# Second layer of a two-layer decoder: stick-breaking queries and keys projected first, scored at every fourth step, GpSimd's small operations on DVE and ACT

## The chip, the cores and the metric

The kernel runs on one core of a Trainium2 chip. The core has a matrix engine (TensorE; its rows in a profile are PE for the matmuls and PEld for the loads of the stationary operand), a vector engine (VectorE, DVE), a scalar engine (ScalarE, ACT), GpSimd (POOL) and SyncE (SP), which here only issues the loads of the weights. Each engine runs its own instructions in the order in which the program lists them, and waits on semaphores for the others. The metric is the device time of one execution, in microseconds (us).

## The reference

Two post-norm layers over 256 positions with a model width of 2048, float32 in and out, causal. Each layer computes `x = LN(alpha*x + mixer(x))` and then `x = LN(alpha*x + relu(x W1)^2 W2)` with a hidden width of 8192. The mixer of the first layer (even) is a sliding-window attention beside a dilated one. The change is in the mixer of the second layer (odd):

```
h = x @ w_in                               # 2048 -> 3*1024 + 512 + 256 + 32
qc, kc, vc, cq, ckv, kr = split(h)
# C: stick-breaking attention, 16 heads of 64
z = qc kc^T / 8 ; strict causal mask
log_keep = log_sigmoid(-z); after = reverse exclusive cumsum of log_keep over keys
oc = exp(log_sigmoid(z) + after) @ vc
# D: latent attention, 16 heads, 64 + 32 (rotary) wide
q  = rms(cq) @ w_uq ; kv = rms(ckv) @ w_ukv
od = softmax([q_nope, rope(q_rope)] . [k_nope, rope(kr)] / sqrt(96)) @ v
y = concat(oc, od) @ w_out
```

## The kernel before

**Precision.** Every large product runs as three float32r products: a weight block `w` is split into `w_hi` (a rounding copy, on ACT, line 120) and `w_lo = w - w_hi` (on DVE, line 121), the activations likewise, and hi*hi, lo*hi and hi*lo are summed in PSUM.

**Units.** All weights come through one `Stream`, in the order in which `plan` (line 380) lists them, as units of 128 x 1024 numbers (512 KB; 384 KB for the queries of D). `Stream.next` hands out one unit; ahead of that it emits the loads (up to five units ahead of the splits) and the split of the unit that stands three later. So each unit costs ACT one `w_hi`, DVE one `w_lo`, and PE 12, 16 or (for `ukv`) 18 matmuls.

**Projections.** `project` (line 833, through `ws`, line 305) computes 512 output columns, transposed, from eight units into four PSUM banks named `acc`; `v_c` (line 894, through `as_`, line 341) computes the values of C from eight units into two such banks; `uq` (line 947) computes the D queries of four heads from two units into four banks, `ukv` (line 980) the D keys and values of eight heads from two units into four banks. There are four `acc` banks in all. A bank is handed on when it has been read: after `project` and `uq` by `join` (line 334), an ACT copy `xfull` and a DVE addition for each bank; after `v_c` by ACT copies; after `ukv` by copies, of which two banks go to ACT and two to DVE (lines 1002 to 1013).

**Attention between the units.** After each unit `pump` (line 189) runs one small piece: a function of the list `late`, a step of a side generator, and one attention step (`attn_step`, line 213). An attention job holds eight heads (half of C or half of D: C0, D0, C1, D1). A step at which a pair of heads is scored emits `qk` (line 682, PE, into two PSUM banks named `sc`, of which there are two) and the mask additions of both heads (DVE; line 1046 for C, 1027 for D). The later stages of a head follow one step apart: for C three ACT activations (`soft`, lines 1050 to 1052), the DVE scans (`sums`, lines 1057 to 1061), an ACT exponential (line 1064); for D maxima on DVE, exponentials on ACT, a division on DVE. Some steps after the scoring, `flip` transposes the weights on PE (line 260) and `weigh` multiplies them with the values (lines 279 and 281). The next pair may be scored two steps later: `self.turn = i + 2` (line 239).

**Order in the second layer** (`odd`, line 841). First the latents `cq` and `ckv, kr`; then values of C0, queries of C0, two units of D queries, keys of C0; from here C0 is scored. Then two units of D queries, values of C1, `ukv`; from here D0 is scored. Then queries of C1, two units of D queries, keys of C1; C1 is scored. Then two units of D queries, `ukv`; D1 is scored. The output projection follows: 16 units for C0 and D0, eight for C1, eight for D1.

**GpSimd.** After each `uq`, `rotate` (line 955) turns the rotary rows of two heads: two DVE multiplications and one addition on GpSimd (line 959). After each `ukv`, GpSimd copies the shared rotary key beside each pair's keys (line 1008, four copies).

Of the kernel before, what the change touches and what calls it, by code (L numbers as in the profile page):

```python
# [15 lines left out]
ALU = mybir.AluOpType  # L16
# [3 lines left out]
S = 256  # L20
D = 2048
# [45 lines left out]
class Stream:  # L67


    def __init__(self, k):  # L70
        self.k = k
        self.units = []
        self.nd = 0
        self.ns = 0
        self.nu = 0
        self.live = {}
# [74 lines left out]
class Job:  # L151


    def __init__(self, name, n, per, score, stages, value, lag, y):
        self.name, self.n, self.per, self.lag = name, n, per, lag
        self.score, self.stages, self.value, self.y = score, stages, value, y
        self.left = n // 2
        self.out = []
        self.s = {}
        self.pt = {}  # L160
        self.o = None


class Trunk:
# [48 lines left out]
    def attn_step(self):  # L213
# [24 lines left out]
        self.todo.popleft()  # L238
        self.turn = i + 2
        scs = [self.ps.tile([P, 384], F32, name="sc", bufs=2) for _ in pair]  # L240
# [139 lines left out]
    def plan(self):  # L380
# [18 lines left out]
        w.block(wi, 0, KT, 3584, 288)  # L399
        w.block(wi, 0, KT, 2048, 512)  # L400
        w.block(wi, 0, KT, 0, 512)
        self.plan_uq(0, 0)
        w.block(wi, 0, KT, 1024, 512)
        self.plan_uq(0, 1)
        w.block(wi, 0, KT, 2048 + 512, 512)
        self.plan_ukv(0)
        w.block(wi, 0, KT, 512, 512)
        self.plan_uq(1, 0)
        w.block(wi, 0, KT, 1024 + 512, 512)
        self.plan_uq(1, 1)  # L410
        self.plan_ukv(1)
        wo = a["odd_w_out"][0]
# [428 lines left out]
    def odd(self):  # L841
# [23 lines left out]
        self.side.append(self.latents(zq, zk, kr))  # L865
        vc0 = self.v_c()
        qc0 = self.project(512, "c", 0.125)
        self.finish_side()
        q0 = self.uq()
        kc0 = self.project(512, "c")  # L870
        c0 = self.job_c("C0", qc0, kc0, vc0, self.y_at)
        q0 += self.uq()
        vc1 = self.v_c()
        d0 = self.job_d("D0", q0, self.ukv(), self.y_at)
        qc1 = self.project(512, "c", 0.125)
        q1 = self.uq()
        kc1 = self.project(512, "c")
        c1 = self.job_c("C1", qc1, kc1, vc1, self.x_slot)
        q1 += self.uq()
        d1 = self.job_d("D1", q1, self.ukv(), lambda k: self.x_slot(4 + k))  # L880
        st = self.new_stats()
        for jobs, first, stats in (((c0, d0), True, None), ((c1,), False, None), ((d1,), False, st)):
# [3 lines left out]
            for c in range(4):  # L886
                end = stats is not None and c == 3
                o = self.as_(xs, len(xs), 512, hold=2 if end else 0)
                if not end:
                    self.add_res(o, c, first, stats)  # L890
                    self.pump()
        return (o, c, False), st

    def v_c(self):
# [52 lines left out]
    def uq(self):  # L947
# [7 lines left out]
        def rotate(q):  # L955
            tmp = self.at.tile([P, 2, S], F32, name="rtmp", bufs=1)
            nc.vector.tensor_tensor(tmp[64:96], q[96:128], sn, op=ALU.mult)
            nc.vector.tensor_tensor(q[64:96], q[64:96], cs, op=ALU.mult)
            nc.gpsimd.tensor_tensor(q[64:96], q[64:96], tmp[64:96], op=ALU.add)

# [19 lines left out]
    def ukv(self):  # L980
# [21 lines left out]
        for f in range(4):  # L1002
            k = self.tile2("d")
            src = banks[f // 2][:, (f % 2) * S:(f % 2) * S + S]
            copy = nc.vector.tensor_copy if f > 1 else nc.scalar.copy
            copy(k[0:64, 0, :], src[0:64, :])
            copy(k[0:64, 1, :], src[64:128, :])
            nc.gpsimd.tensor_copy(k[64:96], self.krT[64:96, :].unsqueeze(1).to_broadcast([32, 2, S]))
            ks.append(k)
# [8 lines left out]
    def job_d(self, name, qs, kv, y):  # L1018
# [13 lines left out]

        job = Job(name, 8, 1, score, (bias, power, divide), value, 5, y)
        self.queue(job)
        return job

    def job_c(self, name, qs, ks, vs, y):
# [30 lines left out]

        job = Job(name, 8, 1, score, (mask, soft, sums, power), value, 6, y)
        self.queue(job)  # L1070
# [97 lines left out]
```

## Time and profile before

| what | value |
|---|---|
| median of 3 runs | 2216.11 us (2214.33 to 2218.61) |
| the profiled execution, own time | 2213.81 us |
| its span, first to last instruction | 2212.0 us |
| mean granted TensorE clock | 0.996 |
| busy, share of the span | PE 98%, PEld 83%, DVE 63%, ACT 48%, POOL 3% |
| the stretch 1185 to 1470 us (the mixer of the second layer) | DVE 9.8 of 10 us busy in 1250 to 1280 and again in 1360 to 1390 |

The profile names instructions by line of the kernel, engine and tile; a wait is put down to the instruction that released it. Tables by windows give the busy time of each engine in each stretch, with the number of instructions in brackets, and at the end the granted TensorE clock, the share of the DMA engines and the moved GB/s. A timeline row gives the start in us, the duration in us, the instruction, and in brackets the idle time of the engine before it and what ended it. The engines overlap neighbouring instructions, so what an instruction costs its engine is read from the distance between two starts.

### The profile page before, as it was taken

To read this page: it belongs to the slowest core of one execution; us is meant where nothing else is said; L and a number is where in the kernel's file an instruction comes from. 1 tells how busy PE (TensorE), PEld (TensorE's weight loads), DVE (VectorE), ACT (ScalarE), POOL (GpSimd) and SP (SyncE) were. 2 spreads that over 40 slices of the span, in tenths; PEclk is the share of its full clock that TensorE was granted. 3 is DMA by queue.
4 is the path that set the end of the run, shared out by engine and by line. 5 is a ranking of instruction groups with operands and counts; after the bars stand their busy time and mean duration, and the time that the engine had idled before them with its cause. 6 is when DMAs were issued, how large, how long until landed. Compare 5 with 4: busy or idle time off the path is not lost.

```text
span 2212.0 us, 30040 instructions
## 1 busy us (share of the span) xinstructions
PE 2177.3 (98%) x11603; PEld 1829.7 (83%) x11604; DVE 1403.4 (63%) x1903; ACT 1058.6 (48%) x1525; POOL 61.0 (3%) x85
## 2 busy tenths in 40 slices
PE   9999999999999999999999999999999999999997
PEld 7888887888888888888888787778888888888885
DVE  5766465775565465556578888878645555655665
ACT  4555453554454354354345566645535534534542
POOL 0000000000000000000022101000000000000001
PEclk9999999999999999999999999999999999999998
DMA  7445554555565555555557544456555556555652
GB/s 265 151 139 158 155 169 158 194 191 200 181 199 192 191 180 198 191 184 188 192 160 212 155 126 144 143 200 212 197 191 177 196 192 189 171 208 173 202 187 105
DMA packets 224320, 399.07 MB, mean 180 GB/s; under 512 B 12778, under 2 KB 56512, under 8 KB 223408
## 3 DMA queue, kind: packets, MB, share of 16 engines
q1 hardware_dynamic: 221760, 387.30, 53.0%
q0 software_dynamic: 2416, 9.84, 1.6%
q8 instruction: 91, 1.49, 0.3%
q14 instruction: 53, 0.43, 0.1%
HBM read 395.00 MB, written 2.10 MB: 180 GB/s over the span
## 4 chain that ended last, share of the span: by engine, by line
PE 61%; issue 31%; DVE 5%; DMA 1%; ACT 1%; POOL 0%; SPq 0%; POOLq 0%; DVEq 0%; ACTq 0%
PE acc L326 14%; PE acc L372 9%; PE acc L374 9%; PE acc L373 9%; PE acc L327 7%; PE sc L326 3%; DVE w_lo L121 2%; PE sc L327 1%; PE o L326 1%; PE pt L326 1%; PE sc L688 1%; PE pt L260 1%; PE o L279 1%; DMA raw<-in_even_w_in 1%; PE o L327 1%
## 5 line engine op out<-in xcount | busy, mean ns | idle before, releaser
L121 DVE TENSOR_TENSOR w_lo<-raw,w_hi 128x1024 fp32r<-128x1024 f32 (+2 forms) x748 | 890.9, 1204 | 610.9 <-ACT w_hi L120 606.7
L120 ACT CAST w_hi<-raw 128x1024 fp32r<-128x1024 f32 (+2 forms) x748 | 759.2, 1028 | 765.3 <-PE acc L374 458.8
L326 PE MATMUL acc<-x,w_hi 128*128 128x512 f32 x1824 | 652.5, 401 | 3.6 <-DVE x L515 3.3
L327 PE MATMUL acc<-x,w_lo 128*128 128x256 f32 x1824 | 512.4, 281 | 0.7 <-DVE w_lo L121 0.7
L326 PEld LDWEIGHTS acc<-x,w_hi 128*128 128x128 f32 x1824 | 343.2, 188 | 89.8 <-issue 3.8
L374 PE MATMUL acc<-w_hi,h_lo 128*128 128x512 f32 x1016 | 398.5, 392 | 0.0
L373 PE MATMUL acc<-w_lo,h_hi 128*128 128x512 f32 x1016 | 398.2, 392 | 0.0
L372 PE MATMUL acc<-w_hi,h_hi 128*128 128x512 f32 x1016 | 396.1, 390 | 0.0
L327 PEld LDWEIGHTS acc<-x,w_lo 128*128 128x128 f32 x1824 | 345.4, 189 | 1.4 <-DVE w_lo L121 1.0
L372 PEld LDWEIGHTS acc<-w_hi,h_hi 128*128 128x128 f32 x1016 | 190.7, 188 | 42.6
L373 PEld LDWEIGHTS acc<-w_lo,h_hi 128*128 128x128 f32 x1016 | 190.8, 188 | 42.4
L374 PEld LDWEIGHTS acc<-w_hi,h_lo 128*128 128x128 f32 x1016 | 190.9, 188 | 40.0
L326 PE MATMUL sc<-x,w_hi 128*128 128x512 f32 x512 | 185.4, 396 | 0.0
L327 PE MATMUL sc<-x,w_lo 128*128 128x256 f32 x512 | 143.4, 280 | 0.0
L372 PE MATMUL acc<-w_hi,x 128*128 128x256 f32 (+2 forms) x400 | 136.3, 341 | 0.3 <-DVE x L514 0.2
L374 PE MATMUL acc<-w_hi,x 128*128 128x256 f32 (+2 forms) x400 | 133.2, 333 | 0.0
L373 PE MATMUL acc<-w_lo,x 128*128 128x256 f32 (+2 forms) x400 | 133.0, 332 | 0.1
L326 PEld LDWEIGHTS sc<-x,w_hi 128*128 128x128 f32 x512 | 96.1, 188 | 23.0
L338 ACT ACTIVATE xfull<-acc 128x256 f32<-128x256 f32 x130 | 49.7, 385 | 126.5 <-PE acc L327 108.9
L327 PEld LDWEIGHTS sc<-x,w_lo 128*128 128x128 f32 x512 | 96.7, 189 | 0.0
L326 PE MATMUL o<-x,w_hi 128*128 128x512 f32 x256 | 95.6, 396 | 0.0
L326 PE MATMUL pt<-x,w_hi 128*128 128x512 f32 x256 | 95.6, 396 | 0.0
(197 smaller groups left out, 2088.6 us busy)
## 6 DMA issues: line engine op xcount, KB each, us to landing
raw<-in_mlp_w SPq DMA_DIRECT2D x512, 512.0 KB, 3.8
raw<-in_even_w_in SPq DMA_DIRECT2D x92, 512.0 KB, 4.2
raw<-in_odd_w_in SPq DMA_DIRECT2D x56, 512.0 KB, 3.6
raw<-in_odd_w_out SPq DMA_DIRECT2D x32, 512.0 KB, 3.4
raw<-in_even_w_out SPq DMA_DIRECT2D x24, 512.0 KB, 3.7
gb_rows<-in_ln_g POOLq DMA_DIRECT2D x3, 1024.0 KB, 4.8
gb_rows<-in_ln_b POOLq DMA_DIRECT2D x3, 1024.0 KB, 6.8
raw<-in_odd_w_uq SPq DMA_DIRECT2D x8, 384.0 KB, 4.0
```

Source lines behind the costliest of these rows:

```text
L120: nc.scalar.copy(h, r)
L121: nc.vector.tensor_tensor(l, r, h.bitcast(F32), op=ALU.subtract)
L260: nc.tensor.transpose(pt[:, b * P:(b + 1) * P], st[:, u * 384 + b * P:u * 384 + (b + 1) * P], self.ident)
L279: nc.tensor.matmul(o[rows, :], v, w[:, 0:S], start=first, stop=False, skip_group_check=True)
L326: nc.tensor.matmul(banks[f], hi[:, c:c + P], both, start=first, stop=False, skip_group_check=True)
L327: nc.tensor.matmul(banks[f][:, S:2 * S], lo[:, c:c + P], xh, start=False, stop=last, skip_group_check=True)
L338: nc.scalar.activation(t, bank[:, S:2 * S], AF.Copy, scale=scale)
L372: nc.tensor.matmul(outs[t], xh[:, ts], hi[:, c:c + width], start=first, stop=False, skip_group_check=True)
L373: nc.tensor.matmul(outs[t], xh[:, ts], lo[:, c:c + width], start=False, stop=False, skip_group_check=True)
L374: nc.tensor.matmul(outs[t], xl[:, ts], hi[:, c:c + width], start=False, stop=last, skip_group_check=True)
L688: nc.tensor.matmul(sc[:, cols], q[:, qs], k[:, ks], start=True, stop=True, skip_group_check=True)
```

## The change

The second layer's loop body becomes one function, `heads(half, ...)`, called twice. In each half the queries and keys of C are projected first, C is queued for scoring, then come the values of C, both groups of D queries (four units in a row), and `ukv`; then D is queued. The list of weight units is put in the same order. `Job` gets a `pace`: pairs of C are scored four steps apart, pairs of D three (the first layer's jobs keep two). The rotary addition goes from GpSimd to DVE, and the copies of the rotary key from GpSimd to ACT.

```diff
--- before.py
+++ after.py
@@ -151,8 +151,8 @@
 class Job:
 
 
-    def __init__(self, name, n, per, score, stages, value, lag, y):
-        self.name, self.n, self.per, self.lag = name, n, per, lag
+    def __init__(self, name, n, per, score, stages, value, lag, y, pace=2):
+        self.name, self.n, self.per, self.lag, self.pace = name, n, per, lag, pace
         self.score, self.stages, self.value, self.y = score, stages, value, y
         self.left = n // 2
         self.out = []
@@ -236,7 +236,7 @@
                 both = self.at.tile([P, 768], F32, name="S", bufs=self.s_bufs)
                 job.s[h], job.s[h + 1] = both[:, 0:384], both[:, 384:768]
         self.todo.popleft()
-        self.turn = i + 2
+        self.turn = i + job.pace
         scs = [self.ps.tile([P, 384], F32, name="sc", bufs=2) for _ in pair]
         self.qk(scs, [job.score(g, u) for g in pair])
         for j, (g, sc) in enumerate(zip(pair, scs)):
@@ -397,18 +397,12 @@
         wi = a["odd_w_in"][0]
         w.block(wi, 0, KT, 3072, 512)
         w.block(wi, 0, KT, 3584, 288)
-        w.block(wi, 0, KT, 2048, 512)
-        w.block(wi, 0, KT, 0, 512)
-        self.plan_uq(0, 0)
-        w.block(wi, 0, KT, 1024, 512)
-        self.plan_uq(0, 1)
-        w.block(wi, 0, KT, 2048 + 512, 512)
-        self.plan_ukv(0)
-        w.block(wi, 0, KT, 512, 512)
-        self.plan_uq(1, 0)
-        w.block(wi, 0, KT, 1024 + 512, 512)
-        self.plan_uq(1, 1)
-        self.plan_ukv(1)
+        for half in range(2):
+            for c0 in (0, 1024, 2048):
+                w.block(wi, 0, KT, c0 + half * 512, 512)
+            self.plan_uq(half, 0)
+            self.plan_uq(half, 1)
+            self.plan_ukv(half)
         wo = a["odd_w_out"][0]
         for k0s in ((0, 8), (4,), (12,)):
             for c in range(4):
@@ -863,21 +857,8 @@
             nc.vector.tensor_tensor(kr[:, t, 64:96], kt_[:, t, :], ks[:, t, :], op=ALU.add)
         self.pump()
         self.side.append(self.latents(zq, zk, kr))
-        vc0 = self.v_c()
-        qc0 = self.project(512, "c", 0.125)
-        self.finish_side()
-        q0 = self.uq()
-        kc0 = self.project(512, "c")
-        c0 = self.job_c("C0", qc0, kc0, vc0, self.y_at)
-        q0 += self.uq()
-        vc1 = self.v_c()
-        d0 = self.job_d("D0", q0, self.ukv(), self.y_at)
-        qc1 = self.project(512, "c", 0.125)
-        q1 = self.uq()
-        kc1 = self.project(512, "c")
-        c1 = self.job_c("C1", qc1, kc1, vc1, self.x_slot)
-        q1 += self.uq()
-        d1 = self.job_d("D1", q1, self.ukv(), lambda k: self.x_slot(4 + k))
+        c0, d0 = self.heads(0, self.y_at, self.y_at)
+        c1, d1 = self.heads(1, self.x_slot, lambda k: self.x_slot(4 + k))
         st = self.new_stats()
         for jobs, first, stats in (((c0, d0), True, None), ((c1,), False, None), ((d1,), False, st)):
             for j in jobs:
@@ -890,6 +871,17 @@
                     self.add_res(o, c, first, stats)
                     self.pump()
         return (o, c, False), st
+
+    def heads(self, half, yc, yd):
+
+        qc = self.project(512, "c", 0.125)
+        kc = self.project(512, "c")
+        vc = []
+        c = self.job_c(f"C{half}", qc, kc, vc, yc)
+        vc += self.v_c()
+        self.finish_side()
+        q = self.uq() + self.uq()
+        return c, self.job_d(f"D{half}", q, self.ukv(), yd)
 
     def v_c(self):
         o = self.as_(self.xT, KT, 512)
@@ -956,7 +948,7 @@
             tmp = self.at.tile([P, 2, S], F32, name="rtmp", bufs=1)
             nc.vector.tensor_tensor(tmp[64:96], q[96:128], sn, op=ALU.mult)
             nc.vector.tensor_tensor(q[64:96], q[64:96], cs, op=ALU.mult)
-            nc.gpsimd.tensor_tensor(q[64:96], q[64:96], tmp[64:96], op=ALU.add)
+            nc.vector.tensor_tensor(q[64:96], q[64:96], tmp[64:96], op=ALU.add)
 
         kt = 0
         for u in range(2):
@@ -1005,7 +997,7 @@
             copy = nc.vector.tensor_copy if f > 1 else nc.scalar.copy
             copy(k[0:64, 0, :], src[0:64, :])
             copy(k[0:64, 1, :], src[64:128, :])
-            nc.gpsimd.tensor_copy(k[64:96], self.krT[64:96, :].unsqueeze(1).to_broadcast([32, 2, S]))
+            nc.scalar.copy(k[64:96], self.krT[64:96, :].unsqueeze(1).to_broadcast([32, 2, S]))
             ks.append(k)
         for b in range(2):
             v = self.tile2("d")
@@ -1030,7 +1022,7 @@
         def value(h, u, blk):
             return vs[h // 4][:, blk, (h % 4) * HD:(h % 4) * HD + HD]
 
-        job = Job(name, 8, 1, score, (bias, power, divide), value, 5, y)
+        job = Job(name, 8, 1, score, (bias, power, divide), value, 5, y, pace=3)
         self.queue(job)
         return job
 
@@ -1066,7 +1058,7 @@
         def value(h, u, blk):
             return vs[h // 4][:, blk, (h % 4) * HD:(h % 4) * HD + HD]
 
-        job = Job(name, 8, 1, score, (mask, soft, sums, power), value, 6, y)
+        job = Job(name, 8, 1, score, (mask, soft, sums, power), value, 6, y, pace=4)
         self.queue(job)
         return job
 
```

How this moves instructions is seen at three places. The first is SP, which issues the weight loads in the order of the units, from the values and projections of C0 on (`odd_w_uq` are the D queries, `odd_w_ukv` the D keys and values, the other `odd_w_in` blocks the projections of C). Before:

```order
L92 DMA raw<-in_odd_w_in 128x2x512 x16
L92 DMA raw<-in_odd_w_uq 128x2x384 x2
L92 DMA raw<-in_odd_w_in 128x2x512 x8
L92 DMA raw<-in_odd_w_uq 128x2x384 x2
L92 DMA raw<-in_odd_w_in 128x2x512 x8
L92 DMA raw<-in_odd_w_ukv 128x1024 x2
L92 DMA raw<-in_odd_w_in 128x2x512 x8
L92 DMA raw<-in_odd_w_uq 128x2x384 x2
L92 DMA raw<-in_odd_w_in 128x2x512 x8
L92 DMA raw<-in_odd_w_uq 128x2x384 x2
L92 DMA raw<-in_odd_w_ukv 128x1024 x2
```

Now:

```order
L92 DMA raw<-in_odd_w_in 128x2x512 x24
L92 DMA raw<-in_odd_w_uq 128x2x384 x4
L92 DMA raw<-in_odd_w_ukv 128x1024 x2
L92 DMA raw<-in_odd_w_in 128x2x512 x24
L92 DMA raw<-in_odd_w_uq 128x2x384 x4
L92 DMA raw<-in_odd_w_ukv 128x1024 x2
```

The eight-unit projections that stood between the groups of D queries are gone from there: four units of queries and two of `ukv` now follow each other.

The second place is DVE behind the second `uq` of the first half, from its joins (`d<-acc,xfull`) on. `rtmp` and `d<-d,rope_f` are the rotation, `sb_a` and `S<-S,sb_a` one head's `sums`, `w_lo` the split of a later unit, `S<-masks,sc` the mask additions. Before (C0's first pair has been scored one step earlier):

```order
L339 SCALAR_TENSOR_TENSOR d<-acc,xfull 128x256 x4
L957 TENSOR_TENSOR rtmp<-d,rope_f 32x512
L958 TENSOR_TENSOR d<-d,rope_f 32x512
L121 TENSOR_TENSOR w_lo<-raw,w_hi 128x1024 x2
L957 TENSOR_TENSOR rtmp<-d,rope_f 32x512
L958 TENSOR_TENSOR d<-d,rope_f 32x512
L1057 SCALAR_TENSOR_TENSOR sb_a<-S,sb_a 128x384
L1060 SCALAR_TENSOR_TENSOR sb_a<-sb_a 128x128
L1060 SCALAR_TENSOR_TENSOR sb_a<-sb_a 128x256
L1061 TENSOR_TENSOR S<-S,sb_a 128x384
L1046 TENSOR_TENSOR S<-masks,sc 128x384 x2
```

Now, behind the joins of the first of the half's two `uq` (lines are those of the changed kernel: 949 to 951 the rotation, 1049 to 1053 the sums, here of C0's fifth head):

```order
L339 SCALAR_TENSOR_TENSOR d<-acc,xfull 128x256 x4
L949 TENSOR_TENSOR rtmp<-d,rope_f 32x512
L950 TENSOR_TENSOR d<-d,rope_f 32x512
L951 TENSOR_TENSOR d<-d,rtmp 32x512
L286 TENSOR_TENSOR y<-o,y 128x256
L121 TENSOR_TENSOR w_lo<-raw,w_hi 128x1024 x2
L949 TENSOR_TENSOR rtmp<-d,rope_f 32x512
L950 TENSOR_TENSOR d<-d,rope_f 32x512
L951 TENSOR_TENSOR d<-d,rtmp 32x512
L1049 SCALAR_TENSOR_TENSOR sb_a<-S,sb_a 128x384
L1052 SCALAR_TENSOR_TENSOR sb_a<-sb_a 128x128
L1052 SCALAR_TENSOR_TENSOR sb_a<-sb_a 128x256
```

The next row is the last of that head's sums, and then come the four joins of the half's second `uq`: they stand behind two rotations with their additions and one head's sums. Behind them come a rotation, the sums of the sixth head, two `w_lo`, another rotation and the masks of C0's fourth pair, and only then DVE's copies out of the banks of `ukv`.

The third place is ACT at that `ukv`: `d<-acc` are its copies out of the banks, `d<-krT` the rotary key, `y<-o` the cast of an attention output, `pT<-pt` a transposed weight block. Before:

```order
L1006 COPY d<-acc 64x256
L1007 COPY d<-acc 64x256
L1006 COPY d<-acc 64x256
L1007 COPY d<-acc 64x256
L1013 COPY d<-acc 128x256 x2
L285 CAST y<-o 128x256
L262 COPY pT<-pt 128x384
L120 CAST w_hi<-raw 128x1024 x2
```

Now:

```order
L998 COPY d<-acc 64x256
L999 COPY d<-acc 64x256
L1000 COPY d<-krT 32x512
L998 COPY d<-acc 64x256
L999 COPY d<-acc 64x256
L1000 COPY d<-krT 32x512 x3
L1005 COPY d<-acc 128x256 x2
L285 CAST y<-o 128x256
L1042 ACTIVATE sb_a<-S 128x384
```

Four copies of the rotary key stand among the copies out of the banks; the two casts `w_hi` that follow now come behind one head's three activations (lines 1042 to 1044).

## The prediction

> **What bounds the kernel now.** I read the page first, then the table of ten-us windows over the second layer's mixer, then its waits, then PE's timeline.
>
> ```profile
> PE 2177.3 (98%) x11603; PEld 1829.7 (83%) x11604; DVE 1403.4 (63%) x1903; ACT 1058.6 (48%) x1525; POOL 61.0 (3%) x85
> ...
> 1250.00:1260.00 10.00, 7.72 (x30) 5.58 (x29) 9.83 (x16) 5.94 (x11) 3.51 (x5) 0.83 0.36 105
> 1320.00:1330.00 10.00, 10.00 (x64) 8.30 (x64) 9.81 (x14) 5.54 (x8) 2.57 (x2) 1.00 0.34 116
> ```
>
> PE is busy nearly everywhere, so only the few us in which it waits can be won, and anything that makes it wait is lost in full. Those waits lie where DVE has no idle time left (9.83 of 10 us): the first pairs of C0 and, a hundred us later, of C1. The waits in 1180 to 1480 us:
>
> ```profile
> DVE w_lo L121 <- ACT w_hi L120: 30.1, 31, 2.0
> ...
> PEld sc L688 <- DVE S L1046: 6.2, 6, 2.7
> PEld acc L996 <- ACT c L900: 0.9, 1, 0.9
> PEld sc L688 <- DVE S L1027: 0.8, 1, 0.8
> PEld acc L372 <- ACT d L1007: 0.6, 1, 0.6
> ```
>
> Scoring waits for the masks of the pair before (only two `sc` banks). PE's timeline prices it:
>
> ```profile
> 1243.80 0.39 PE L374 MATMUL acc<-w_hi,x 128*128 128x512 f32 x1
> 1244.12 0.93 PE L688 MATMUL sc<-c 64*128 64x128 f32 x8
> 1244.98 0.50 PE L372 MATMUL acc<-w_hi,x 128*128 128x512 f32 x1
> ...
> 1250.33 0.39 PE L374 MATMUL acc<-w_hi,x 128*128 128x512 f32 x1
> 1253.00 1.39 PE L688 MATMUL sc<-c 64*128 64x128 f32 x8 [2.28 <-DVE S L1046]
> 1254.31 0.50 PE L372 MATMUL acc<-w_hi,x 128*128 128x512 f32 x1
> ...
> 1255.29 0.63 PE L372 MATMUL acc<-w_hi,x 128*128 128x512 f32 x1
> 1255.72 0.63 PE L373 MATMUL acc<-w_lo,x 128*128 128x512 f32 x1
> ...
> 1362.34 0.39 PE L374 MATMUL acc<-w_hi,y 128*128 128x512 f32 x1
> 1364.52 1.39 PE L688 MATMUL sc<-c 64*128 64x128 f32 x8 [1.79 <-DVE S L1046]
> 1365.83 0.50 PE L372 MATMUL acc<-w_hi,y 128*128 128x512 f32 x1
> ...
> 1368.70 0.39 PE L372 MATMUL acc<-w_hi,y 128*128 128x512 f32 x1
> 1370.63 0.50 PE L373 MATMUL acc<-w_lo,y 128*128 128x512 f32 x1 [1.54 <-DVE w_lo L121]
> ...
> 1373.26 0.49 PE L260 MATMUL pt<-ident,S 128*128 128x128 f32 x3
> ...
> 1375.64 0.50 PE L372 MATMUL acc<-w_hi,y 128*128 128x512 f32 x1
> ```
>
> A free scoring takes 1.18 us from the matmul before to the one behind (1243.80 to 1244.98), a blocked one 3.98, 3.49 and 2.38: 2.80, 2.31 and 1.20 lost. The late `w_lo` costs 1.93 - 0.23 = 1.70 (0.23 is the distance back to back). After the first gap the granted clock falls (0.83 over the window): eight matmuls of 512 columns stand 0.43 apart instead of 0.23, 1.6 us. With 0.9 + 0.8 + 0.6 from the waits the stage loses 11.9; about 0.3 of that is an ordinary switch, so **11.6 us** is all that could come back.
>
> **What the change removes.** (a) The score waits: pairs stand four steps apart, and C's first two pairs fall beside the values of C, where DVE has only splits. (b) GpSimd's hold on DVE:
>
> ```profile
> 1248.73 0.56 DVE L1057 SCALAR_TENSOR_TENSOR sb_a<-S,sb_a 128x384 f32<-128x384 f32 x1
> ...
> 1252.40 1.00 DVE L1046 TENSOR_TENSOR S<-masks,sc 128x384 f32<-128x384 f32 x2
> ...
> 1257.74 0.55 DVE L1057 SCALAR_TENSOR_TENSOR sb_a<-S,sb_a 128x384 f32<-128x384 f32 x1
> ...
> 1259.84 1.01 DVE L1046 TENSOR_TENSOR S<-masks,sc 128x384 f32<-128x384 f32 x2
> 1260.77 1.22 DVE L121 TENSOR_TENSOR w_lo<-raw,w_hi 128x1024 fp32r<-128x1024 f32 x1
> ```
> ```profile
> 1250.39 3.12 POOL L1008 COPY d<-krT 32x512 f32<-32x512 f32 x4
> ```
>
> One head's sums take 3.67 us while GpSimd copies (1248.73 to 1252.40) and 2.10 free (1257.74 to 1259.84). I credit the whole 11.6 to these two (bounds: at the least the three blocked scorings and the clock, 7.9, if the other waits come back elsewhere; 11.6 at the most). What must be priced is what comes in its place. The order of the weight loads moves as well, but no row of the stage has PE, DVE or ACT wait for a load, and the number of units between loads and use is unchanged: nothing. C0's and D1's last heads are still multiplied well ahead of their output projection: nothing.
>
> **What it adds.** The additions are eight more DVE instructions, the copies eight more on ACT. The nearest rows:
>
> ```profile
> 1238.36 0.50 PE L969 MATMUL acc<-y,w_hi 128*128 128x512 f32 x1
> ...
> 1242.33 0.69 DVE L957 TENSOR_TENSOR rtmp<-d,rope_f 32x512 f32<-32x512 f32 x1
> 1243.03 0.68 DVE L958 TENSOR_TENSOR d<-d,rope_f 32x512 f32<-32x512 f32 x1
> ...
> L959 POOL TENSOR_TENSOR d<-d,rtmp 32x512 f32<-32x512 f32 x8 | 12.9, 1612 | 161.3 <-DVE d L958 153.3 <-ACT pT L262 4.2 <-ACT d L1013 3.8
> L262 ACT COPY pT<-pt 128x384 f32<-128x384 f32 x32 | 15.4, 480 | 11.7 <-PE pt L260 11.0
> L1006 DVE COPY d<-acc 64x256 f32<-64x256 f32 x4 | 1.6, 412 | 0.0
> ```
>
> An addition of that shape is taken at 0.70 (bounds: 0.68, the multiplication's own duration, and 1.6 as on GpSimd; nearest is the former, DVE's own row of that shape), a rotation then 2.1. A copy on ACT of 512 columns is taken at 0.5 start to start (0.38 to 0.6 around the row of 384 columns). By count that is 5.6 us of DVE and 4 us of ACT in 285 us: hidden behind PE's matmuls if it were spread, for both engines wait for each other or for PE elsewhere (the first row of the waits); without cover all 5.6 would count. The additions fall where DVE is full, and this is the step that decides.
>
> **Four units of D queries, then `ukv`, on four banks.** Each of these blocks needs all four `acc` banks, so PE waits for the joins of the one before, and joins stand in DVE's queue behind rotations, splits and sums. I keep account of one half from the first matmul of the first `uq`'s second unit, t = 0. PE: a unit 2.84, a weigh 0.9, a flip 0.3, a scoring 0.95, a `ukv` unit 2.85, from
>
> ```profile
> 1206.27 0.48 PE L969 MATMUL acc<-y,w_hi 128*128 128x512 f32 x1
> ...
> 1212.00 0.39 PE L326 MATMUL acc<-x,w_hi 128*128 128x512 f32 x1
> ...
> 1296.79 0.65 PE L279 MATMUL o<-pT,c 128*64 128x256 f32 x4
> ```
>
> (two query units 5.73; a weigh's four longer products 0.65, its four shorter ones and the switch taken as 0.25; flip and `ukv` unit are estimates by columns). PE would be ready for `ukv` at 2.84 + 0.9 + 2.84 + 0.3 + 2.84 + 0.3 = 10.0.
>
> DVE: as in the rows above, the four joins end and the rotation starts at 4.0; rotation to 6.1; attention output 6.4; the two splits wait for ACT, which has one head's activations first:
>
> ```profile
> 1257.15 0.51 ACT L1050 ACTIVATE sb_a<-S 128x384 f32<-128x384 f32 x1
> ...
> 1258.67 1.03 ACT L120 CAST w_hi<-raw 128x1024 fp32r<-128x1024 f32 x1
> ```
>
> 1.5 of activations and 1.0 of cast after ACT's joins (3.5) and output cast (4.2) give 6.9; two splits at 1.13 (1260.77 follows 1259.84 by 0.93, the mask pair) to 9.1; rotation 11.2; sums 13.3; first join 13.7. **PE waits 10.0 to 13.8.** Then, on DVE: three joins 15.1, rotation 17.2, sums 19.3, two splits 21.6, rotation 23.7, masks 24.6, four copies 26.3. PE: `ukv`, scoring, `ukv`, weigh to 21.3. The next block's banks come free in the order of their copies: two from ACT, which after its exponential at 19.7 needs four copies, four of the rotary key and two more (22.0 and 24.0), two from DVE (26.3 and on). In the first half a projection takes all four: its unit ends at 26.35 + 1.4 = 27.75 instead of 20.4, **7.35 late**. In the second half the output projection takes the first two: 24.05 + 2.05 = 26.1 instead of 20.3, **5.8 late**. Sum 13.1. Behind it the splits catch up: the unit two later starts at 31, its `w_lo` is done at 28.3.
>
> **The clock.** One drop like the 1.6 above is added, for the broken stretch at 21 to 26 in the first half. The Trainium skill ("TensorE: Matmul & The Clock Gate", Part 1) says that the clock halves after an idle window of about 3.4 us. The rows differ: a gap of 2.28 did it, 1.79 did not. By the skill only the first wait of each half (3.8) would halve it, and there the later wait takes it up; the sum would be 1.6 less.
>
> **Sum**, against the profiled execution's own 2213.8: - 11.6 + 13.1 + 1.6 = + 3.1, 2216.9. That execution lay 2.3 below the median of the runs shown, 2216.1, so the predicted median is **2219.2**. About 0.2% (4.4 us) is what a measurement of this kernel can tell from no change; the forecast lies inside it.
>
> **Rivals.**
> *Slower: DVE's queue is longer than counted.* PE waits on that queue in full, so every us on it is lost from the first one on. Two things would lengthen it at once. The additions could lie half-way to their mean on GpSimd, at 1.15: four stand ahead of the last copies of each half, + 1.8. And DVE could stand idle ahead of splits whose cast is late: it did so 31 times in the stage, 30.1 us together, one us a time, and the account has only one such wait, of half a us, in each half: + 0.7 for a second. Together 2.5 us per half: 2224. Beyond 2.7, the margin of the split due at 31, a third wait would follow. Against it: the multiplications of the same shape cost 0.70, and the other three splits find ACT ahead of DVE in my account.
>
> *Faster: the hand-overs cost little.* In 1320 to 1330 a group of D queries hands its banks to a projection amid D0's attention without a us of PE idle (the window above). If DVE reached the joins within 2 us of the data, each half would lose some 2 us: - 11.6 + 4 gives 2208.5. It needs DVE's queue between two sets of joins to be 6.8 us shorter than I count, the sums and both rotations. Against: in that window no scans stand between.
> *It does not do what it says:* the order shows the moves, so no chance is kept for it.
>
> **How the numbers follow.** The forecast has 0.52, with its own range 2216 to 2223 (no drop or three, additions at the bounds); slower 0.32; faster 0.16. Slower by over 0.2% (above 2220.5): 0.29 of the rival's and 0.11 of the forecast's, 0.40. Faster by over 0.2% (below 2211.7): 0.13. Within: 0.47. The range runs from 2210 to 2227.
>
> **What would show it.** Right: waits of `sc` on the masks gone; in each half PE waiting about 3.7 us at the first `ukv` matmul for a join (line 339), and about 4 and 2.5 us in pieces at the unit after `ukv`, for copies on ACT and DVE; head sums at 2.1 throughout; DVE without idle time for some 22 us there. Wrong: if PE passes the first `ukv` matmul freely, the count of DVE's queue is wrong; if the stretch from the first joins to the last copy on DVE is well over 22 us, or PE waits for a `w_lo` behind it, the slower rival holds.

## The result, and the profile after

The changed kernel takes 2224.99 us (median of 6 runs, 2220.39 to 2226.06), the kernel before 2216.01 beside it (6 runs, 2214.33 to 2218.61). The ratio is 1.0041, 95% interval 1.0031 to 1.0051: **slower by 0.4%, some 9 us**. The predicted median was 2219.2, the forecast lay within 0.2%; the whole range, 2210 to 2227, holds the result, but only by the slower rival's part of it: the forecast's own range, 2216 to 2223, does not.

The profiled execution of after took 2226.06 us (span 2224.3), 12.25 more than that of before. Not all of this is the change. The two do the same up to the second layer, and yet the first matmul behind the latents (the first unit of the part that was reordered) starts 3.37 us later in after. A shift of 0.7 to 3.5 us, most of it from the first layer, stands in every profiled execution below, whichever order the kernel has, so it is the profile of before that was early there. I therefore compare a stretch that is the same work in all kernels, called **the mixer** below: from that matmul to the first transposition of the layer norm behind the mixer. PE's timeline of before:

```profile
1159.95 0.40 PE L372 MATMUL acc<-w_hi,x 128*128 128x512 f32 x1
...
1476.95 0.33 PE L502 MATMUL sc<-ident,x_res 128*128 128x128 f32 x1 [0.71 <-DVE x_res L599]
```

and of after:

```profile
1163.32 0.40 PE L326 MATMUL acc<-x,w_hi 128*128 128x512 f32 x1
...
1489.60 0.33 PE L496 MATMUL sc<-ident,x_res 128*128 128x128 f32 x1 [0.71 <-DVE x_res L593]
```

317.00 against 326.28: the mixer is **9.3 us longer**, close to the 9.0 between the medians. PE's waits in after, 1150 to 1480 us:

```profile
PE acc L982 <- DVE d L339: 7.0, 2, 3.5
PE acc L326 <- DVE krs L856: 3.6, 1, 3.6
PE acc L372 <- ACT d L1005: 0.8, 1, 0.8
PE acc L326 <- ACT d L1005: 0.8, 1, 0.8
PE acc L326 <- DVE d L999: 0.8, 1, 0.8
```

No scoring (`sc`) waits for masks any more. (A row gives the sum of the waits in us, their number and the longest.) The first row is the predicted wait at the first `ukv` matmul (predicted 3.8 in each half), the last three are the predicted hand-over behind `ukv`. The second row is in no part of the prediction: `krs` is the rotary part of the key latent, which DVE reads out of two `acc` banks at the very start of the mixer. PE there:

```profile
1164.60 0.28 PE L327 MATMUL acc<-x,w_lo 128*128 128x256 f32 x1
1168.50 0.77 PE L326 MATMUL acc<-x,w_hi 128*128 128x512 f32 x1 [3.62 <-DVE krs L856]
...
1173.71 0.39 PE L326 MATMUL acc<-x,w_hi 128*128 128x512 f32 x1
```

The step from 1164.60 to 1168.50 should be 0.11: 3.79 lost. Then eight pairs of matmuls take 5.21 instead of 8 x 0.355, since the granted clock has fallen: 2.37 lost. **6.2 us** together, against 0.3 in before on its unit there (at 1168.69, one step of 0.54 instead of 0.23): 5.9 more. Why DVE was late shows in its own timeline:

```profile
1165.28 1.22 DVE L121 TENSOR_TENSOR w_lo<-raw,w_hi 128x1024 fp32r<-128x1024 f32 x1
...
1167.48 0.61 DVE L906 TENSOR_SCALAR d<-d,rs 128x256 f32<-128x256 f32 x2 [0.90 <-POOL rs L566]
...
1168.29 0.19 DVE L856 TENSOR_TENSOR krs<-krs,rope_t 128x32 f32<-128x32 f32 x1
```

PE had finished the latents at 1163.3, but the reading of the rotary columns is emitted behind the normalization of the latents, and that behind a split and behind GpSimd's `rs`. In before the next block was the values of C, which needs two banks, and two were free. In after it is the queries of C, which needs four.

The predicted places, first half (PE, then DVE):

```profile
1244.71 0.50 PE L961 MATMUL acc<-y,w_hi 128*128 128x512 f32 x1
...
1254.60 0.49 PE L260 MATMUL pt<-ident,S 128*128 128x128 f32 x3
1258.62 0.38 PE L982 MATMUL acc<-y,w_hi 128*128 128x256 f32 x1 [3.52 <-DVE d L339]
...
1269.56 0.49 PE L326 MATMUL acc<-x,w_hi 128*128 128x512 f32 x1 [0.80 <-ACT d L1005]
1271.31 0.50 PE L326 MATMUL acc<-x,w_hi 128*128 128x512 f32 x1 [0.79 <-DVE d L999]
```
```profile
1248.70 0.69 DVE L949 TENSOR_TENSOR rtmp<-d,rope_f 32x512 f32<-32x512 f32 x1
...
1250.12 0.68 DVE L951 TENSOR_TENSOR d<-d,rtmp 32x512 f32<-32x512 f32 x1
1250.83 0.42 DVE L286 TENSOR_TENSOR y<-o,y 128x256 fp32r<-128x256 f32 x1
...
1256.04 0.56 DVE L1049 SCALAR_TENSOR_TENSOR sb_a<-S,sb_a 128x384 f32<-128x384 f32 x1
...
1258.15 0.75 DVE L339 SCALAR_TENSOR_TENSOR d<-acc,xfull 128x256 f32<-128x256 f32 x2
...
1269.54 0.41 DVE L998 COPY d<-acc 64x256 f32<-64x256 f32 x1
```

With t = 0 at 1244.71, as in the prediction, DVE's rotation starts at 4.0 (predicted 4.0), the next join begins at 13.4 (13.3) and ends so that PE starts `ukv` at 13.9 (13.8); DVE's copies begin at 24.8 (the end of the masks, 24.6). The table by windows shows how the granted clock fell behind the waits (its column stands before the last two):

```profile
1160.00:1170.00 10.00, 6.38 (x40) 5.76 (x39) 8.84 (x33) 4.54 (x9) 4.68 (x9) 0.84 0.95 282
1170.00:1180.00 10.00, 10.00 (x49) 8.58 (x49) 7.12 (x17) 3.15 (x3) 4.27 (x8) 0.82 0.92 214
...
1260.00:1270.00 10.00, 9.20 (x52) 6.91 (x52) 9.74 (x16) 7.43 (x16) 0.00 (x0) 0.88 0.34 104
1370.00:1380.00 10.00, 7.57 (x34) 6.21 (x35) 9.59 (x17) 3.93 (x8) 0.00 (x0) 0.66 0.09 35
```

It fell three times, each time right behind a wait of over 3.5 us.

### The profile page after: what moved, and what is told of

Its sections match the earlier page's. It is cut to its first block, busy times and chain, and to the rows that moved or that the text cites. A ratio compares the mean times of both kernels' runs of the same rounds, so it can differ in the third digit from the quotient of the medians.

```text
span 2224.3 us, 30021 instructions
## 1 busy us (share of the span) xinstructions
PE 2182.4 (98%) x11603; PEld 1832.6 (82%) x11604; DVE 1401.4 (63%) x1911; ACT 1065.0 (48%) x1533; POOL 41.9 (2%) x69
## 4 chain that ended last, share of the span: by engine, by line
PE 64%; issue 30%; DVE 3%; DMA 1%; ACT 1%; POOL 0%; SPq 0%; POOLq 0%; DVEq 0%; ACTq 0%
PE acc L326 14%; PE acc L372 10%; PE acc L374 10%; PE acc L373 9%; PE acc L327 7%; PE sc L326 3%; PE sc L682 2%; PE sc L327 2%; PE o L326 2%; PE pt L326 2%; PE pt L260 1%; PE o L279 1%; DVE w_lo L121 1%; PE o L327 1%; PE pt L327 1%
```

## Experiments

All times are medians; "against before" is the difference to the kernel before measured beside it on the same chip (its median 2216.77 for the first four kernels, 2216.26 for the next four, 2214.61 for the last four), then the ratio's 95% interval, then how much longer or shorter the mixer is in the profiled execution than the 317.00 of before, from the same two rows.

| kernel | median, us | against before | ratio, 95% | mixer |
|---|---|---|---|---|
| after | 2224.99 | +9.0 | 1.0031 to 1.0051 | +9.3 |
| e1: after, rotary columns copied by ACT | 2219.76 | +3.0 | 1.0004 to 1.0022 | +2.8 |
| e9: after, C0's values first | 2224.75 | +8.5 | 1.0024 to 1.0049 | +9.9 |
| e2: after, GpSimd's operations back | 2224.80 | +8.0 | 1.0019 to 1.0038 | +7.6 |
| e11: order alone | 2218.67 | +4.1 | 1.0008 to 1.0025 | +6.5 |
| e12: e1 without the pace | 2217.48 | +2.9 | 1.0004 to 1.0022 | +0.9 |
| e5: e1, rotations behind `ukv` | 2218.47 | +2.2 | 1.0004 to 1.0022 | +3.2 |
| e6: e1, key rows copied last | 2218.91 | +4.3 | 1.0008 to 1.0025 | +1.9 |
| e3: before, operations moved | 2214.35 | -2.4 | 0.9980 to 0.9997 | -2.5 |
| e4: before, pace | 2215.37 | -1.4 | 0.9982 to 1.0000 | -2.9 |
| e7: before, operations and pace | 2209.79 | -6.5 | 0.9956 to 0.9981 | -3.7 |
| e13: before, operations, key rows last | 2212.22 | -2.4 | 0.9983 to 1.0000 | -2.8 |
| e10: e13 with the pace | 2206.94 | -9.3 | 0.9942 to 0.9970 | -6.7 |

Each mixer is that of one execution. Those profiled of e7 and e10 were the slowest of five and that of after the slowest of six, that of e1 the fastest of eleven, so a mixer says less than a median, and a us between two mixers says little.

### The wait on the rotary columns

My theory once I had the trace: the prediction's own mechanism (a block that needs four banks behind a reader that is late) at a place it had not looked at. Against it stood that the loss might lie in the hand-overs, or that the wait moves on. **e1** lets ACT, which is idle there, copy the 32 columns out first:

```diff
         for t in range(2):
+            nc.scalar.copy(kr[:, t, 64:96], ck[t][:, 256:288])
+        for t in range(2):
             rt = self.rope_t[:, t, :]
-            nc.vector.tensor_copy(ks[:, t, 0:16], ck[t][:, 272:288])
+            nc.vector.tensor_copy(ks[:, t, 0:16], kr[:, t, 80:96])
...
-            nc.vector.tensor_tensor(kt_[:, t, :], ck[t][:, 256:288], rt[:, 0:32], op=ALU.mult)
+            nc.vector.tensor_tensor(kt_[:, t, :], kr[:, t, 64:96], rt[:, 0:32], op=ALU.mult)
```

> The changed kernel, but ACT copies the 32 rotary columns of the key latent out of their two PSUM banks before DVE turns them. Theory (a wait that the prediction left out): the first unit behind the latents now needs four banks, and two of them are held until DVE has read the rotary columns (PE waits 3.6 us, then runs some 4.7 us at a lower clock). With the copy the wait falls to under 1 us and the clock stays up: 5 to 6 us less than the changed kernel, about 2219.5, some 3.5 above the kernel before. Rival: the loss lies elsewhere (the first layer, in which the changed kernel was 3.4 us later in its profiled execution, or the hand-overs): 2224 to 2225, and the wait merely moves.

2219.76, 3.0 above before instead of 9.0. The wait is now 0.6, nothing of the clock's fall is left there, and the rows of the hand-over are as they were:

```profile
PE acc L984 <- DVE d L339: 7.0, 2, 3.5
...
PE acc L326 <- ACT kr L852: 0.6, 1, 0.6
```

So some 6 of the 9 us hang on two PSUM banks that were read too late, and 3 are left for everything that the prediction priced, against its 3.1. (By the mixers, with the reservation above, 6.5 and 2.8.)

**e9** goes round the same wait in the other way: the first block is again the one with two banks.

```diff
-            for c0 in (0, 1024, 2048):
+            for c0 in ((0, 1024, 2048) if half else (2048, 0, 1024)):
...
+        vc = [] if half else self.v_c()
         qc = self.project(512, "c", 0.125)
         kc = self.project(512, "c")
-        vc = []
         c = self.job_c(f"C{half}", qc, kc, vc, yc)
-        vc += self.v_c()
+        if half:
+            vc += self.v_c()
```

> The changed kernel, but in the first half C's values come ahead of its queries and keys, as in the kernel before. Theory (banks of the latents): the unit behind the latents needs two banks that have long been read, so the wait on the rotary columns and its clock drop go, as with the copy on ACT: 2219 to 2220. Rival: C's first scorings now fall beside the four units of D queries, and their sums lengthen DVE's queue ahead of ukv: the wait there grows by a pair's sums, 2 to 4 us, 2222 to 2224.

The wait on `krs` is gone as expected, and yet 2224.75: the rival, a little above its range. The waits:

```profile
PE acc L983 <- DVE d L339: 8.1, 2, 4.5
PE acc L326 <- ACT d L1006: 1.4, 1, 1.4
PE acc L372 <- ACT d L1006: 1.4, 1, 1.4
PE acc L372 <- ACT d L1000: 1.0, 1, 1.0
PE acc L326 <- DVE d L1000: 1.0, 1, 1.0
```

The wait at `ukv` grows from 3.5 to 4.5 in the first half, the hand-over from 2.4 to 4.8 in both halves together, and the clock falls four times there instead of twice. But the rival's way is not the one that the trace shows. PE in e9, from t = 0 as above, and DVE's first join:

```profile
1234.37 0.50 PE L962 MATMUL acc<-y,w_hi 128*128 128x512 f32 x1
...
1247.59 0.58 PE L983 MATMUL acc<-y,w_hi 128*128 128x256 f32 x1 [4.48 <-DVE d L339]
```
```profile
1247.12 0.75 DVE L339 SCALAR_TENSOR_TENSOR d<-acc,xfull 128x256 f32<-128x256 f32 x2
```

DVE's queue is not longer: the join comes at t = 12.75, in after at 13.4. PE has less to do meanwhile: it is ready at 8.7 instead of 10.4, for with the values ahead no head of C0 has come to its flip or weigh by then. So values behind the keys leave flips and weighs of C0 to PE while DVE catches up. The second half has the order of after, but other attention steps fall beside its `ukv`, and its hand-over grew as well. Nothing here tests (a) of the prediction: e9 has no scoring wait for masks either.

### The three parts of the change by themselves

**e2** takes the two moved operations back; **e3** makes them alone, in the kernel before.

```diff
-            nc.vector.tensor_tensor(q[64:96], q[64:96], tmp[64:96], op=ALU.add)
+            nc.gpsimd.tensor_tensor(q[64:96], q[64:96], tmp[64:96], op=ALU.add)
...
-            nc.scalar.copy(k[64:96], self.krT[64:96, :].unsqueeze(1).to_broadcast([32, 2, S]))
+            nc.gpsimd.tensor_copy(k[64:96], self.krT[64:96, :].unsqueeze(1).to_broadcast([32, 2, S]))
```

> The changed kernel with the rotary additions and the copies of the rotary key back on GpSimd: order and pace alone. Theory (GpSimd's hold on DVE, as in the prediction): eight DVE additions less (5.6 us), but head sums of 3.7 instead of 2.1 us beside GpSimd; in each half one or two such sums lie between two sets of joins, so PE waits at the first ukv matmul about 1 us longer and behind ukv another 1 to 2: 2227 to 2230. Rival: what DVE gets back by the additions is as much as it loses: 2224 to 2226, waits within 0.5 us of 3.7.

2224.80: the rival, no difference from after that could be told. DVE's timeline of e2 ahead of `ukv` shows the exchange:

```profile
1254.53 0.56 DVE L1049 SCALAR_TENSOR_TENSOR sb_a<-S,sb_a 128x384 f32<-128x384 f32 x1
1255.13 1.95 DVE L1052 TENSOR_TENSOR_SCAN sb_a<-sb_a 128x128 f32<-128x128 f32 x2
1257.11 0.56 DVE L1053 TENSOR_TENSOR S<-S,sb_a 128x384 f32<-128x384 f32 x1
```
```profile
1254.59 1.62 POOL L951 TENSOR_TENSOR d<-d,rtmp 32x512 f32<-32x512 f32 x1 [3.85 <-DVE d L950]
```

The second rotation's addition has left DVE's queue (0.71 less), and the two scans beside GpSimd's addition take 1.95 instead of the 1.01 that they take in after: 0.94 more. Net 0.23, and the wait at `ukv` is 3.76 instead of 3.52. The first rotation's addition has left it too, but brings nothing: the splits behind it wait for ACT's cast, 0.98 instead of 0.27.

> The kernel before with only the additions on DVE and the copies on ACT. Theory: the first blocked scorings of each half lose GpSimd's hold (sums 3.67 to 2.10, four or five such in each half), the waits of scoring on masks fall from 6.3 to 2 or 3 us in all and the first clock drop goes: about 2211. Rival: the waits come from two sc banks and a pair at every second step, whatever GpSimd does; the additions on DVE take what is won: 2215 to 2217.

2214.35, 2.4 less than before, between the two: the interval, 0.7 to 4.4 less, leaves out both the theory's 5.8 and no change at all. The waits on C's masks fell from 6.2 us in `PEld`'s row to 3.0, but others came up, for ACT, which now copies more:

```profile
PE acc L996 <- ACT c L900: 1.8, 1, 1.8
PE sc L688 <- DVE S L1046: 1.5, 2, 1.0
...
PE acc L372 <- ACT d L1013: 1.4, 1, 1.4
```

**e4** is the pace alone (`pace=4` for C, `pace=3` for D, as in the change's first and last hunks).

> The kernel before with only the pace: C's pairs four steps apart, D's three. Theory: the score waits (2.80, 2.31 and 1.20) and the clock drop go whatever GpSimd does, since the masks of a pair have four units of time: 2208 to 2210. Rival: the same DVE work lies in the same units, only later, and falls on the ukv copies and the weight splits: 2213 to 2216, with waits for a w_lo or an acc bank in place of those for the masks.

2215.37: the rival. The scoring waits are all gone, and the same DVE work (sums, the copies of `ukv`) now stands ahead of splits, one of them 2.8 us late:

```profile
PE acc L373 <- DVE w_lo L121: 3.8, 4, 2.8
```

**e11** is the order alone: the change without the two moved operations and with all pairs two steps apart.

> The kernel before with the order of the change alone: GpSimd keeps its operations and pairs stay two steps apart. Theory (the order alone carries all that is lost: wait on the rotary columns 5.5, two waits ahead of ukv of 3.8, hand-over and clock 5, against the score waits of 8 that go since C's first pairs lie beside its values): 2222 to 2225, as with order and pace together (8.0 above). Rival: at two steps the pairs wait for their masks beside GpSimd as in the kernel before, so the order adds its loss to those waits: 2228 to 2232.

4.1 above before, less than either said; the kernel before was faster on this chip, so the bare 2218.67 says little. The trace has no scoring wait, so the rival falls: beside the values of C, pairs two steps apart do not wait. It has the other waits of the theory, the ones at `ukv` smaller than the 3.8 that I expected:

```profile
PE acc L982 <- DVE d L339: 5.7, 2, 2.9
PE acc L326 <- DVE krs L856: 4.0, 1, 4.0
```

**e12** is e1 with all pairs two steps apart (the two `pace=` arguments taken out).

> The changed kernel with the rotary columns copied by ACT and with all pairs two steps apart again. Theory (pace is of no use in this order): all four pairs of C are scored beside its values, where DVE has only splits, so no score waits come up; the waits ahead of ukv stay (one head's sums lie there either way), but sums and masks are gone from the hand-over behind ukv: 1 to 3 us less, 2216.5 to 2218.5. Rival (the prediction's): pairs two steps apart wait for the masks of the pair before, 1 to 3 us each: 2221 to 2225.

2.9 above before, the same as e1's 3.0, so the theory's gain of 1 to 3 us doesn't show in the medians, though 2217.48 lies in its range (before was faster on this chip; the mixer is 1.9 shorter than e1's). In the new order the pace is worth nothing that could be measured, and it isn't needed, for no scoring waits for masks. So the rival falls. The waits are 3.3 at `ukv` and 0.5 twice behind it.

### Can the waits around `ukv` be moved away?

**e5** puts the rotations of a half behind `ukv` (on top of e1):

```diff
-                        self.late.append(lambda q=q: rotate(q))
+                        later.append(lambda q=q: rotate(q))
...
-        q = self.uq() + self.uq()
-        return c, self.job_d(f"D{half}", q, self.ukv(), yd)
+        later = []
+        q = self.uq(later) + self.uq(later)
+        kv = self.ukv()
+        self.late.extend(later)
+        return c, self.job_d(f"D{half}", q, kv, yd)
```

> The changed kernel with the rotary columns copied by ACT (as in the run of that name, 3.0 us above the kernel before) and with all four rotations of a half emitted behind ukv instead of between the D queries. Theory (the wait at the first ukv matmul is DVE's queue between two sets of joins, sums and both rotations): 4.2 us leave that queue, the two waits of 3.5 fall to under 0.5 each, and with the clock drops behind them 8 to 9 us come back: about 2210 to 2212, 5 below the kernel before. Rival: the rotations then stand before the splits and copies behind ukv, and PE waits there instead, for DVE's copies, a w_lo or a scoring of D: gain under 3 us, 2217 to 2219.

The rival. The wait at `ukv` falls from 3.5 to 1.3 (not to nothing: DVE then idles 2.05 us ahead of the two splits, which wait for ACT's casts), and comes back as waits for ACT, whose exponentials of D wait for DVE's maxima, and these stand behind the postponed rotations:

```profile
PE pt L260 <- ACT pT L262: 6.2, 2, 3.1
PE acc L987 <- DVE d L339: 2.6, 2, 1.3
PE acc L326 <- DVE c L339: 2.0, 2, 1.7
```

**e6** puts ACT's copies of the rotary key behind its copies of the values (on top of e1):

```diff
-            nc.scalar.copy(k[64:96], self.krT[64:96, :].unsqueeze(1).to_broadcast([32, 2, S]))
             ks.append(k)
...
             vs.append(v)
+        for k in ks:
+            nc.scalar.copy(k[64:96], self.krT[64:96, :].unsqueeze(1).to_broadcast([32, 2, S]))
         self.pump()
```

> The changed kernel with the rotary columns copied by ACT, and with ACT's copies of the rotary key moved behind its copies of ukv's values. Theory (the hand-over behind ukv waits for banks that ACT reads late, as the prediction has it): the waits for line 1007, about 0.9 in each half, go, and those for DVE's copies stay: 1.5 to 2 us below the 3.0 above the kernel before, 2217.5 to 2218. Rival: DVE's copies end as late as ACT's, so PE waits for them instead: within 0.7 us of 2219.3.

No gain that could be told, although before was 2 us faster on this chip than on e1's: the rival. The rows for ACT's copies are gone, the one for DVE's copy (line 1001, 0.7) stays: there, in the first half, it is DVE that is late.

**e7** and **e10** are the change without its order: before with the moved operations and the pace, and the same with the key rows last.

> The kernel before with the pace and with GpSimd's operations on DVE and ACT, in the order before: all of the change but the order. Theory of the prediction (both together take all 11.6 us away, and only the order costs): 2206 to 2208. Theory after the two single runs (2.4 and 1.4 below): each wait removed lets another engine's come up, so the two add at most: 2212 to 2214, with waits left for ACT's copies (lines 900, 1007, 1013) and a late w_lo. Rival: they remove the same waits: 2214 to 2215.

> As the run with pace and moved operations in the order before, but ACT copies the rotary key behind the values of ukv instead of between the keys. Theory (ACT's copies hold ukv's banks): the banks are free four copies (some 2 us) earlier, the waits for lines 1007 and 1013 go: 1.5 to 2.5 us below that run. Rival: the next unit then waits for DVE's copies of ukv or for a w_lo: within 0.7 us of it.

e7 took 2209.79, 6.5 below before: more than e3 and e4 together by the medians (3.8, with intervals that reach 4 each), less than the prediction's credit, between the first two theories. e10 took 2206.94, 9.3 below (ratio 0.9956, 0.9942 to 0.9970): **the lowest median of all, below both kernels**. That is 2.9 below e7, in the direction of its theory and a little more than that said, but the intervals of the two overlap. The waits speak for the theory: with the pace the order of ACT's copies counts. e7's waits on ACT, and what is left of them in e10:

```profile
PE acc L372 <- ACT d L1013: 1.4, 1, 1.4
PE acc L372 <- ACT d L1007: 1.1, 1, 1.1
PE acc L326 <- ACT d L1007: 1.1, 1, 1.1
```
```profile
PE acc L373 <- DVE w_lo L121: 1.7, 1, 1.7
...
PE acc L326 <- ACT d L1007: 0.5, 1, 0.5
PE acc L372 <- ACT d L1007: 0.5, 1, 0.5
```

**e13** is e10 without the pace.

> The kernel before, its order and its pace, with GpSimd's operations on DVE and ACT and the copies of the rotary key behind those of the values: the fastest version so far (9.3 below the kernel before) without its pace. Theory (the pace is worth some 4 us once GpSimd is off, as the step from 2.4 to 6.5 below says): 2210 to 2212, with score waits on masks of 2 to 3 us in all. Rival: the late banks of ukv were all, and the pace is worth under 1.5 us: 2207 to 2208.5.

2212.22, just above the theory's range, and 2.4 below before as e3: without the pace the place of the key rows is worth nothing that could be measured (`sc` waits 2.5 in all, one for `w_lo` of 1.5, one of 1.8 for ACT's line 900), and the pace is worth 4 us by the mixers, 7 by the medians on two chips, so the rival falls.

## Why the prediction was right or wrong

**What bounds it now, 11.6 us.** Right in kind: the scoring waits for masks are gone in after. Of (a) and (b) as causes the runs keep (a): order alone removes the scoring waits (e11), and so does pace alone (e4). (b), GpSimd's hold on DVE, is real but small: e3 gains 2.4, and in the new order the two moved operations give and take the same (e2). The size was never measured by itself; without the order 9.3 came back (e10). It was also a little too large: three of its waits (0.9, 0.8, 0.6) are `PEld`'s, and PE's own rows for them are 0.7, 0.6 and 0.2, which makes 10.8.

**"Four units of D queries, then `ukv`, on four banks": right, nearly row for row.** The first waits are 3.5 and 3.5 (3.8), the additions 0.71 start to start (0.70), sums 2.11 (2.10); ACT's rotary copies took 0.55 to 0.62, not 0.5. (The first split, which the account has at 6.9 though its own terms add up to 6.7, started at 6.8.) The unit behind `ukv` ends at t = 28.0 in the first half (1271.31 plus the 1.4 that the prediction has behind the last bank) and at 28.15 in the second (the same t = 0 at 1358.53, the unit's end at 1386.68), where it would end unhindered at 20.4 and 20.3: 7.6 + 7.85 = 15.4 lost, against 13.1 + 1.6 = 14.7. In its parts the account was less good: PE came to the unit behind `ukv` later than predicted (at 23.1, not 21.3, in the first half), and its waits there are 1.6 and 0.8, not 4 and 2.5.

**The clock** was put in the wrong place. It fell behind the first wait of each half, on `ukv` itself, not behind it, and twice, not once. In the first half PE's slower `ukv` only used up part of the hand-over's wait: the unit ends at 28.0 beside the 27.75 that the prediction had before it added 1.6. In the second it lasted for all eighteen matmuls of a `ukv` unit, 2.2 us more (4.85 from the first start to the last, 1372.43 to 1377.28, against 2.63 for the next unit), and the end is 2.05 behind the predicted 26.1. The Trainium skill ("TensorE: Matmul & The Clock Gate", Part 1) has this fall at the first waits; the saving of 1.6 that I worked out from it did not come, since the second half paid.

**The step that failed** is the one that applied bank hand-over only where D queries meet `ukv`. "Each of these blocks needs all four `acc` banks, so PE waits for the joins of the one before" holds as well for the first block of the first half: the change puts the queries of C, four banks, in the place of the values of C, two banks, straight behind the latents, whose rotary columns DVE reads last. Moving the values was costed for weight loads and for the multiplication of the heads, and called nothing. It cost 5.9 us: -11.6 + 15.4 + 5.9 = 9.7, against the 9.3 measured. Without it the forecast was 3.1 for a kernel that was measured 3.0 above before (e1). That both sums come out to within half a us is in part luck: with PE's own rows in the credit they would be 10.5 and, with the measured 15.4, 4.6.

**The rivals.** The slower one named 2224, near the result, for the wrong reason: additions did not take 1.15, and DVE idled 0.27 ahead of a late split in the first half, where the account had half a us and the rival 0.7 more. So it is luck that the range held. The faster one falls: the hand-overs cost what was counted. (The sums and both rotations that it needed gone are 6.3 us by the account's own rows, not 6.8.)

**What stays open.** Whether e7 gains more than e3 and e4 together is not settled by the intervals, and why it should is only read from the waits (each alone lets another engine's wait come up). Whether the pace costs anything in the new order isn't settled: e11 against e2 says 4 us, but on two chips with overlapping intervals, and e12 against e1 says none.

## What to carry to other kernels

When blocks of work are reordered, list for each new neighbour pair how many PSUM banks the later one needs, and which engine reads them last behind the earlier one, for the first block too and not only where the queue looks full. A bank should be read by the engine that is idle, ahead of work that needs no bank: here two ACT copies of 32 columns were worth some 6 us. And parts of a change are worth measuring apart: the pace and the moved operations gave 6.5 us, 9.3 with the copies put right, and the order took more than that away.

## What the runs showed of the hardware that I had not expected

Two scans on DVE (128x128, then 128x256) take 1.01 us alone and 1.95 to 1.98 beside a GpSimd addition of 32x512 (four of four in e2). The 128x384 operation ahead of them, also beside that addition, kept its 0.56; but it had started 0.06 us before GpSimd did, and the addition took 1.62 instead of the 1.28 to 1.30 that it takes otherwise in that half. So it isn't shown whether the kind of operation decides or which of the two starts first.

The clock fell behind every wait of PE of 3.29 us or more (15 of 15 in the mixers of these profiles, for 2.5 to 6 us: matmuls of 512 columns stand 0.43 us apart there instead of 0.23). That is about what the Trainium skill ("TensorE: Matmul & The Clock Gate", Part 1) says of an idle window. Shorter waits decided nothing by their length: behind waits of 2.28 (before), 2.80 and 2.89 (both e11) and 3.10 (e5) it fell, behind 2.84 (e4) and 3.07 (e5) it did not, and in e7 it fell behind one of 1.39 that followed another of 1.14 two us before.
